# A residual block in fp32 on one core: seven block products for eight in six blocks of the last FFN

## The chip, the core and the metric

The kernel runs on one core of a Trainium2 chip. The time is the device time of one execution in microseconds (us); three executions of the kernel before are given. Engines are named as in the profile: PE (TensorE, matmuls; PEld its weight loads), DVE (VectorE), ACT (ScalarE), POOL (GpSimd) and SP (SyncE, whose queue issues nearly all loads).

## The reference

One layer of a streaming encoder, batch 1, 256 tokens, model width 2048, all in float32. Three sublayers follow one another: an FFN, a mixer (mLSTM heads and RG-LRU channels), and an FFN again. The last is the one that changes:

```python
def _swiglu(u, w13, w2):
    g, v = jnp.split(u @ w13, 2, axis=-1)
    return (jax.nn.silu(g) * v) @ w2
...
mod = (jax.nn.silu(c) @ w_ada[l] + b_ada[l]).reshape(B, N_SUBLAYERS, 3, D_MODEL)
shift, scale, gate = mod[:, :, 0], mod[:, :, 1], mod[:, :, 2]
...
y = _swiglu(modulate(x, 2), ffn2_w13[l], ffn2_w2[l])
x = _layer_norm(ALPHA * x + FFN_WEIGHT * gate[:, 2, None, :] * y, ln_g[l, 2], ln_b[l, 2])
```

`modulate` is a layer norm without gain, times 1 + scale, plus shift. w13 is 2048 x 11264 (5632 columns of g and as many of v), w2 is 5632 x 2048.

## The kernel before

Float32 products are made of three matmuls in a rounded float32 format: each operand is split into a high and a low part, and high x high, high x low and low x high are added in PSUM (`mov_t`, L295). A weight tile is 128 partitions x 2048, 1 MB: 512 rows of K by 512 columns. `load` (L82) has SP fetch it into one of four raw buffers; `split` (L89) has ACT cast it into the high part and DVE subtract that from the raw tile for the low part, in one of three buffer pairs. PE then does 24 matmuls with it: two token halves of 128 (`t`), four K steps of 128, three terms. The activations lie in SBUF as `u2`, transposed and split already (`uh`, `ul`), and are the stationary operand.

The FFN works in blocks of 512 columns of g and the same 512 of v. `rows_block` (L591) does one block: four tiles of K for g, four for v, two PSUM banks each (`fg`, `fv`), then silu(g) x v on ACT and DVE, eight transposes on PE and another split (`gated` L611, `turn` L621) into `hth`, `htl`. Two blocks are a group; there are 11 blocks and six groups, 0 to 5. `g2` (L770) multiplies a group's result with its eight w2 tiles, two for each 512 output columns, and adds the sum into `yacc` in SBUF. In the last FFN the loop at L815 runs `g1(gi)`, the blocks of a group, and then `g2(gi-1)`. The last group but one and the last go through `g2_kept` and `boundary` (L360), which end the kernel.

The vector `mod` comes from 142 further 1 MB tiles, `w_ada`, each a DVE reduction against `scb` (silu(c) on all partitions). `load` calls `tick` (L194), which lets in such an ada tile at a rate per weight tile; for the last FFN this rate is `FFN2_RATE`, and 16 tiles, those of its gate, are left to do there. `gate_rows` (L201) turns the 16 results into a row by a PE transpose, a POOL transfer to DRAM and another back to all partitions, into `gate`. `scale_x` multiplies x by ALPHA on ACT; `residual` (L339) adds gate x yacc to x on DVE.

The order on each engine is set when the program is built, by a scheduler that keeps data dependencies; each engine, and SP's queue, then runs its list strictly in order, and waits where an entry's operand isn't ready.

Of the kernel before, what the change touches and what calls it, by code (L numbers as in the profile page):

```python
# [2 lines left out]

# [13 lines left out]
P = 128  # L17
D = 2048
# [18 lines left out]
RAMP_RATE = (0.75, 0.67, 0.88, 0.6)  # L37
FFN1_RATE = 0.74
MIX_RATE = dict(o=1.2, x=0.8, g=0.4, v=0.4, k=1.25, q=0.5, heads=0.0, out=1.0)
FFN2_RATE = 0.3  # L40

MOD_ACT = (3, 2)

# [8 lines left out]
def block_kernel(ctx: ExitStack, tc: tile.TileContext, a: dict, out: bass.AP):  # L52
# [9 lines left out]
    def slot(name, dtype=F32):  # L62

        return ph.tile([P, SLOT], dtype, tag="slot", bufs=6, name=name)
# [5 lines left out]
    def bank(name):  # L70
        return psp.tile([P, 512], F32, tag="ps", name=name)

    def raw_tile(name):
        return wp.tile([P, 2048], F32, tag="raw", bufs=4, name=name)
# [14 lines left out]
    def split(tile, act, low):  # L89

        raw, name, into = tile
        hi, lo = into() if into else [wp.tile([P, 2048], F32R, tag=w, bufs=3, name=w[0] + name) for w in ("hi", "lo")]
        step = 512 if fine[0] else 2048
        cols = [slice(c, c + step) for c in range(0, 2048, step)]
        for w in cols:
            act.copy(cut(hi, w), like(raw[:, w], hi))  # L96
        for w in cols:
            low.tensor_sub(cut(lo, w), like(raw[:, w], lo), cut(hi, w).bitcast(F32))  # L98
        return hi, lo

    def load_w(src, name, into=None):

        return split(load(src, name, into), nc.scalar, nc.vector)
# [52 lines left out]
            nc.tensor.transpose(ps[:, k * P:(k + 1) * P], col[:, k:k + 1].to_broadcast([P, P]), ident)  # L156


    scb = big.tile([P, D], F32, name="scb")
    sc = cst.tile([P, KT], F32, name="sc")  # L160
    nc.scalar.dma_start(sc, a["c"])
    nc.scalar.activation(sc, sc, AF.Silu)
    for n in range(4):
        ps = bank(f"pc{n}")
        rows_of(ps, sc[:, 4 * n:4 * n + 4])
        nc.scalar.copy(scb[:, n * 512:(n + 1) * 512], ps)
    x = big.tile([P, NT, D], F32, name="x")


    u2 = big.tile([P, KT, 2, S], F32R, name="u2")  # L170
# [2 lines left out]
    badac = cst.tile([P, 3, 3, KT], F32, name="badac")  # L173
    adac = cst.tile([P, 3, 3, KT], F32, name="adac")
    modc = adac[:, :, 0:2, :]
    gate = big.tile([P, D], F32, name="gate")


    todo = list(enumerate(_ada_tiles()))
# [9 lines left out]
    def ada_until(s, j, kt):  # L189

        while any(key == (s, j, kt) for _, key in todo):
            ada_tile()
# [8 lines left out]
    def gate_rows(s, weight):  # L201

        pt = bank(f"adag{s}")
        nc.tensor.transpose(pt[0:KT, 0:P], adac[:, s, 2, :], ident)
        row = sm.tile([KT, P], F32, tag="grow", bufs=1, name=f"grow{s}")
        nc.scalar.mul(row, pt[0:KT, 0:P], weight)
        line = dram.tile([1, D], F32, name=f"line{s}")
        nc.gpsimd.dma_start(line.rearrange("o (k p) -> (o k) p", p=P), row)
        nc.gpsimd.dma_start(gate, line.to_broadcast([P, D]))
# [85 lines left out]
    def mov_t(ps, hl, acth, actl, k0, t, first, last, te=nc.tensor, part=slice(0, 512)):  # L295

        hi, lo = hl
        tk = slice(t * P, (t + 1) * P)
        for j in range(4):
            w = slice(j * 512 + part.start, j * 512 + part.stop)  # L300
            o = like(ps[:, part], hi)
            te.matmul(o, acth[:, k0 + j, tk], cut(hi, w), start=first and j == 0, stop=False)  # L302
            te.matmul(o, acth[:, k0 + j, tk], cut(lo, w), start=False, stop=False)  # L303
            mm = te.matmul(o, actl[:, k0 + j, tk], cut(hi, w), start=False, stop=last and j == 3)  # L304
        return mm
# [3 lines left out]
    def later(tiles, work):  # L309

        pend.append([tiles, work])

    def tile_done(mm):

        for p in pend:
            p[0] -= 1
        while pend and pend[0][0] <= 0:
            with tc.issue_after(mm.ins):
                pend.pop(0)[1]()
# [5 lines left out]
    def mov_w(pss, hl, acth, actl, k0, first, last):  # L325
        for t in range(NT):
            mm = mov_t(pss[t], hl, acth, actl, k0, t, first, last)
        tile_done(mm)
        return mm
# [18 lines left out]
    def scale_x():  # L348
        for t in range(NT):
            A.mul(x[:, t, :], x[:, t, :], ALPHA)  # L350
# [227 lines left out]
        return [sm.tile([P, 5, 6], F32, tag="sts", bufs=2, name=f"sts{s}{t}") for t in range(NT)]  # L578

    def ffn(s, w13, w2, start, following=None):  # L580
        yacc = [slot(f"yacc{t}")[:, 0:D] for t in range(NT)]
        groups = [list(range(g, min(g + GRP, NFF))) for g in range(0, NFF, GRP)]
        hts = {}
# [4 lines left out]
        def new_h(gi):  # L588
            hts[gi] = [slot(f"{w}{gi}", F32R)[:, 0:GRP * S].rearrange("p (a b) -> p a b", a=GRP) for w in ("hth", "htl")]

        def rows_block(b, pg=None, first=None):  # L591

            i = 8 * (b - b0)
            if pg is None:
                pg = [bank(f"fg{s}{b}{t}") for t in range(NT)]
                for k in range(4):
                    mov_w(pg, load_w(w13[i + k], f"fg{s}_{b}{k}"), uh, ul, k * 4, k == 0, k == 3)
            pv = [bank(f"fv{s}{b}{t}") for t in range(NT)]
            for k in range(4):
                if first and k == 0:  # L600
                    tile = first
                else:
                    tile = load(w13[i + 4 + k], f"fv{s}_{b}{k}")
                    with marked():
                        tile = split(tile, nc.scalar, nc.vector)
                mov_w(pv, tile, uh, ul, k * 4, k == 0, k == 3)
            if 4 * b // GRP not in hts:
                new_h(4 * b // GRP)
            gated(b, pg, pv)
# [137 lines left out]
        def g1(gi):  # L747
            grp = groups[gi]
            if start and gi in (2, 3):
                new_h(gi)  # L750
                b = 2 * gi
                later(1, lambda: turn(b, sgs[b]))
                later(3, lambda: turn(b + 1, sgs[b + 1]))
                if gi == 3:
                    later(3, fetch)
                return
            for b in range(grp[0] // 4, grp[-1] // 4 + 1):
                if b or start:
                    rows_block(b)
# [10 lines left out]
        def g2(gi):  # L770
# [3 lines left out]
            for n in range(4):  # L774
# [6 lines left out]
                for t in range(NT):  # L781
                    if gi == 0:
                        evac.append(nc.scalar.copy(yacc[t][:, c], pss[t]))
                    else:
                        nc.vector.tensor_add(yacc[t][:, c], yacc[t][:, c], pss[t])

        ps_last = {}
        behind_t = []

# [15 lines left out]
        if start is not None:  # L805
            ramp(start)
            credit[:] = 0.0, FFN1_RATE
            done = 2
            g2(0)
            flush()  # L810
        else:
            pg, first = nxt.pop()
            credit[:] = -4.0, FFN2_RATE
            rows_block(0, pg, first)
        for gi in range(done, len(groups)):  # L815
            g1(gi)
            if gi == 2 and not start:
                scale_x()
            if gi == len(groups) - 2:
                ada_until(s, 2, KT - 1)  # L820
                gate_rows(s, 0.5)
            if gi == len(groups) - 1:
                g2_kept(gi - 1)
            elif gi:
                g2(gi - 1)
                if gi == len(groups) - 2:
                    for t in range(NT):
                        for n in range(4):
                            residual(s, t, n, yacc[t][:, n * 512:(n + 1) * 512], None)
# [459 lines left out]
```

## Time and profile before

| | |
|---|---|
| median of 3 executions | 1905.65 us (1905.43 to 1908.52) |
| profiled execution | 1905.46 us, its span 1903.7 us |
| busy: PE / PEld / DVE / ACT / POOL | 98% / 81% / 74% / 44% / 2% |
| mean PE clock granted | 0.998 |
| read from HBM, written | 512.36 MB, 2.12 MB |

Busy is the time in which an engine has at least one instruction under way, as a share of the span. PE's matmuls overlap one another, so the sum of their durations is longer than its busy time. In a row of a group of instructions stand the source line, the engine, the operation, what it writes and reads, how often, then its busy time, the mean of one, and the engine's idle time ahead of it with what ended that.

### The profile page before, as it was taken

How to read it: one execution, taken by the hardware profiler on the slowest of the kernel's cores; microseconds unless marked ns; L12 is line 12 of the kernel's file. 1: busy time of each engine (PE TensorE's matmuls, PEld its weight loads, DVE VectorE, ACT ScalarE, POOL GpSimd, SP SyncE). 2: the span in 40 equal slices, each digit the busy share in tenths (PEclk: the TensorE clock that was granted, in tenths of full speed). 3: DMA queues.
4: the chain of work that ended last, by engine and by line, in shares of the span. 5: the costliest groups of instructions: out<-in, count | busy, mean ns of one | idle time of the engine just before them, and what ended most of it. 6: DMA issues, size and time to landing. Idle time of an engine off the chain costs nothing.

```text
span 1903.7 us, 21169 instructions
## 1 busy us (share of the span) xinstructions
PE 1868.8 (98%) x8555; PEld 1540.9 (81%) x8555; DVE 1416.9 (74%) x1358; ACT 845.0 (44%) x792; POOL 43.1 (2%) x64
## 2 busy tenths in 40 slices
PE   6999999999999999999999999999999999999997
PEld 5888888888888888688888786888888888888886
DVE  7899988879877988897998877455655644545657
ACT  5533444443434335657634247434434334343340
POOL 0000000000000000000000120000000000000000
PEclk9999999999999999999999999999999999999999
DMA  9889977888988886696698664566666655555552
GB/s 365 345 331 361 344 291 306 304 352 317 359 344 336 331 338 235 241 347 241 265 360 326 244 268 156 213 224 244 245 260 245 226 196 193 185 197 202 196 218 92
DMA packets 73202, 515.87 MB, mean 271 GB/s; under 512 B 8544, under 2 KB 8720, under 8 KB 11024
## 3 DMA queue, kind: packets, MB, share of 16 engines
q1 hardware_dynamic: 70848, 507.54, 71.1%
q10 hardware_dynamic: 1728, 3.80, 0.6%
q0 software_dynamic: 528, 3.17, 0.4%
q8 instruction: 67, 1.10, 0.2%
q14 instruction: 31, 0.25, 0.0%
HBM read 512.36 MB, written 2.12 MB: 270 GB/s over the span
## 4 chain that ended last, share of the span: by engine, by line
PE 87%; DVE 6%; ACT 2%; DMA 2%; issue 2%; POOL 0%; DVEq 0%; SPq 0%; ACTq 0%
PE py L302 6%; PE py L303 6%; PE py L304 6%; PE fv L302 5%; PE fv L303 5%; PE fv L304 5%; PE fg L302 5%; PE fg L304 5%; PE fg L303 5%; PE rp L690 5%; PE rp L691 4%; PE rp L692 4%; PE pj L291 4%; PE tl L304 3%; PE tl L302 3%; PE tl L303 3%
## 5 line engine op out<-in xcount | busy, mean ns | idle before, releaser
L186 DVE CUSTOM_DVE_ANT_0 ada<-ada,scb,badac 128x2048 f32<-128x2048 f32 x142 | 333.1, 2346 | 22.7 <-DMA ada<-in_w_ada 22.6
L98 DVE TENSOR_TENSOR lw<-rw,hw 128x2048 fp32r<-128x2048 f32 x80 | 183.3, 2291 | 109.5 <-ACT hw L96 109.2
L96 ACT CAST hw<-rw 128x2048 fp32r<-128x2048 f32 x80 | 153.1, 1914 | 238.7 <-PE py L304 128.7
L98 DVE TENSOR_TENSOR lfv<-rfv,hfv 128x2048 fp32r<-128x2048 f32 x55 | 126.0, 2292 | 127.6 <-ACT hfv L96 127.6
L302 PE MATMUL py<-hw,hth 128*128 128x512 f32 x512 | 200.0, 391 | 0.0
L304 PE MATMUL py<-hw,htl 128*128 128x512 f32 x512 | 199.3, 389 | 0.0
L303 PE MATMUL py<-lw,hth 128*128 128x512 f32 x512 | 199.2, 389 | 0.0
L96 ACT CAST hra<-rra 128x2048 fp32r<-128x2048 f32 x63 | 120.6, 1916 | 161.3 <-PE rp L692 112.4
L98 DVE TENSOR_TENSOR lfg<-rfg,hfg 128x2048 fp32r<-128x2048 f32 x52 | 119.1, 2291 | 95.7 <-ACT hfg L96 95.6
L96 ACT CAST hfg<-rfg 128x2048 fp32r<-128x2048 f32 x52 | 99.5, 1914 | 173.7 <-PE fv L304 74.1
L691 PE MATMUL rp<-lra,u 128*128 128x512 f32 x448 | 174.2, 389 | 1.0 <-DVE lra L98 1.0
L96 ACT CAST hfv<-rfv 128x2048 fp32r<-128x2048 f32 x55 | 105.2, 1914 | 156.8 <-PE fg L304 118.0
L692 PE MATMUL rp<-hra,u 128*128 128x512 f32 x448 | 173.6, 389 | 0.0
L690 PE MATMUL rp<-hra,u 128*128 128x512 f32 x448 | 170.8, 392 | 1.7 <-ACT u L259 1.7
L304 PE MATMUL fv<-hfv,u 128*128 128x512 f32 x440 | 171.2, 389 | 0.0
L303 PE MATMUL fv<-lfv,u 128*128 128x512 f32 x440 | 171.2, 389 | 0.0
L302 PE MATMUL fv<-hfv,u 128*128 128x512 f32 x440 | 171.0, 389 | 0.0
L98 DVE TENSOR_TENSOR lra<-rra,hra 128x2048 fp32r<-128x2048 f32 x63 | 144.2, 2289 | 27.5 <-ACT hra L96 27.3
L302 PE MATMUL fg<-hfg,u 128*128 128x512 f32 x416 | 162.3, 390 | 0.0
L304 PE MATMUL fg<-hfg,u 128*128 128x512 f32 x416 | 161.9, 389 | 0.0
L303 PE MATMUL fg<-lfg,u 128*128 128x512 f32 x416 | 161.9, 389 | 0.0
L291 PE MATMUL pj<-u,hs 128*128 128x512 f32 x512 | 123.0, 392 | 0.3 <-ACT hs L96 0.2
(392 smaller groups left out, 3340.9 us busy)
## 6 DMA issues: line engine op xcount, KB each, us to landing
ada<-in_w_ada SPq DMA_DIRECT2D x142, 1024.0 KB, 5.1
rw<-in_w SPq DMA_DIRECT2D x80, 1024.0 KB, 5.0
rra<-in_w_r SPq DMA_DIRECT2D x64, 1024.0 KB, 5.1
rfg<-in_w SPq DMA_DIRECT2D x55, 1024.0 KB, 4.9
rfv<-in_w SPq DMA_DIRECT2D x55, 1024.0 KB, 4.8
rs<-in_w_s SPq DMA_DIRECT2D x32, 1024.0 KB, 7.0
rwo<-in_w_out SPq DMA_DIRECT2D x16, 1024.0 KB, 4.9
rv<-in_w_vo SPq DMA_DIRECT2D x8, 1024.0 KB, 4.8
```

What stands on the lines that cost most here:

```text
L96: act.copy(cut(hi, w), like(raw[:, w], hi))
L98: low.tensor_sub(cut(lo, w), like(raw[:, w], lo), cut(hi, w).bitcast(F32))
L186: vec.tensor_tensor_reduce(raw, raw, scb, 1.0, badac[:, s, j, kt:kt + 1], ALU.mult, ALU.add, adac[:, s, j, kt:kt + 1])
L291: nc.tensor.matmul(ps, hi[:, w], u2[:, k].rearrange("p w b -> p (w b)"), start=k == 0, stop=False)
L302: te.matmul(o, acth[:, k0 + j, tk], cut(hi, w), start=first and j == 0, stop=False)
L303: te.matmul(o, acth[:, k0 + j, tk], cut(lo, w), start=False, stop=False)
L304: mm = te.matmul(o, actl[:, k0 + j, tk], cut(hi, w), start=False, stop=last and j == 3)
L690: nc.tensor.matmul(pss[t], uh[:, k0 + j, tk], hi[:, w], start=a0 and j == j0, stop=False)
L691: nc.tensor.matmul(pss[t], uh[:, k0 + j, tk], lo[:, w], start=False, stop=False)
L692: mm = nc.tensor.matmul(pss[t], ul[:, k0 + j, tk], hi[:, w], start=False, stop=a1 and j == j0 + nj - 1)
```

## The change

In groups 2, 3 and 4 of the last FFN (`MIXED`), so in blocks 4 to 9, `mixed` takes the place of `rows_block`. Of a block's eight w13 tiles four, the first 1024 rows of K for g and v, are multiplied by Strassen's method in Winograd's form. The activations for these rows are a 2 x 2 matrix of parts: two token halves by two K halves of 512. The weights are one as well: two K halves by the columns of g and of v. The eight products of a part with a part (12 matmuls each) become seven, `q1` to `q7`, of which four have sums of activation parts as one operand and four have combined weights. `token_sums` makes the activation sums once, in group 1; they lie in the place of x. The weight combinations are made in each block, in place in the four raw tiles `r`, which `fetch_w` loads one block ahead: `r[0]` into `scb`, `r[1]` into `gate`, the other two into raw buffers. Each operand of a product is split by itself. The other four tiles (`plain`) are done as before. The products' sums go together in SBUF (`wa`, `wb`, `za`, `zb`).

The eight w2 tiles of the group before no longer follow the two blocks; `mixed` takes one at each of four places in each block. Since the sums need x's place, x goes to DRAM behind block 0 and comes back after block 9, and is scaled and given its residual there. Since `scb` and `gate` hold weights, all ada tiles have to be done before group 2 (`FFN2_RATE` 0.58), and the gate row is made after block 9.

```diff
--- before.py
+++ after.py
@@ -37,7 +38,9 @@
-FFN2_RATE = 0.3
+FFN2_RATE = 0.58
+MIXED = (2, 3, 4)
@@ -156,7 +159,7 @@
-    scb = big.tile([P, D], F32, name="scb")
+    scb = big.tile([P, D], F32, tag="scb", name="scb")
@@ -164,7 +167,7 @@
-    x = big.tile([P, NT, D], F32, name="x")
+    x = big.tile([P, NT, D], F32, tag="x", name="x")
@@ -173,7 +176,7 @@
-    gate = big.tile([P, D], F32, name="gate")
+    gate = big.tile([P, D], F32, tag="gate", name="gate")
@@ -578,6 +581,7 @@
     def ffn(s, w13, w2, start, following=None):
+        nonlocal x, gate
         yacc = [slot(f"yacc{t}")[:, 0:D] for t in range(NT)]
         groups = [list(range(g, min(g + GRP, NFF))) for g in range(0, NFF, GRP)]
         hts = {}
@@ -784,6 +788,141 @@
+        def w2_tile(gi, n, k, pss):
+            hth, htl = hts[gi]
+            kg = 2 * gi + k
+            if k == 0:
+                pss[n] = [bank(f"py{gi}_{n}_{t}") for t in range(NT)]
+            mov_w(pss[n], load_w(w2[kg * 4 + n], f"w2{s}_{kg}_{n}"), hth, htl, k * 4, k == 0, k == 1)
+            if k:
+                c = slice(n * 512, (n + 1) * 512)
+                for t in range(NT):
+                    nc.vector.tensor_add(yacc[t][:, c], yacc[t][:, c], pss[n][t])
+        parts = []
+        def token_sums():
+            home = big.tile([P, 2, KT, P], F32R, tag="x", name="sums")
+            ah = raw_tile("usum").rearrange("p (k b) -> p k b", k=8)
+            nc.vector.tensor_add(ah, uh[:, 0:8, :].bitcast(F32), ul[:, 0:8, :].bitcast(F32))
+            a11, a12, a21, a22 = (ah[:, k:k + 4, t * P:(t + 1) * P] for t in range(NT) for k in (0, 4))
+            ss = raw_tile("ssum").rearrange("p (k b) -> p k b", k=KT)
+            s1, s2, s3, s4 = (ss[:, 4 * i:4 * i + 4, :] for i in range(4))
+            nc.vector.tensor_add(s1, a21, a22)
+            nc.vector.tensor_sub(s2, s1, a11)
+            nc.vector.tensor_sub(s3, a11, a21)
+            nc.vector.tensor_sub(s4, a12, s2)
+            sh, sl = home[:, 0], home[:, 1]
+            nc.scalar.copy(sh, ss)
+            nc.vector.tensor_sub(sl, ss, sh.bitcast(F32))
+            parts[:] = sh, sl
+        held = {}
+        def fetch_w(b, j):
+            tag = {0: "scb", 1: "gate"}.get(j)
+            nm = f"b{b}_{j}"
+            t = big.tile([P, 2048], F32, tag=tag, name=nm) if tag else raw_tile(nm)
+            nc.sync.dma_start(t, w13[8 * b + (0, 4, 1, 5)[j]])
+            held[b, j] = t
+        def mixed(b, ws, more):
+            sh, sl = parts
+            r = [held.pop((b, j)) for j in range(4)]
+            def parted(j, nm):
+                return split((r[j], f"{nm}{s}_{b}", None), nc.scalar, nc.vector)
+            def product(ps, hl, acth, actl, k0, t, first, last):
+                tile_done(mov_t(ps, hl, acth, actl, k0, t, first, last))
+            def plain(pss, k, at, first, last):
+                tile_k = load_w(w13[8 * b + at + k], f"f{s}_{b}{at}{k}")
+                for t in range(NT):
+                    mm = mov_t(pss[t], tile_k, uh, ul, 4 * k, t, first[t], last[t])
+                tile_done(mm)
+            def part_bank(nm):
+                return bank(f"{nm}{s}_{b}")
+            def half_tile(tag, nm):
+                return sm.tile([P, 512], F32, tag=tag, bufs=2, name=f"{nm}{s}{b}")
+            sub = nc.vector.tensor_sub
+            add = nc.vector.tensor_add
+            p1 = part_bank("m1")
+            product(p1, parted(0, "q1"), uh, ul, 0, 0, True, True)
+            next(ws)()
+            g = [part_bank("fg0"), part_bank("fg1")]
+            v = [part_bank("fv0"), None]
+            product(g[0], parted(2, "q2"), uh, ul, 4, 0, True, False)
+            plain(g, 2, 0, (False, True), (False, False))
+            product(v[0], parted(3, "q3"), sh, sl, 12, 0, True, False)
+            sub(r[0], r[1], r[0])
+            sub(r[1], r[3], r[1])
+            sub(r[3], r[3], r[0])
+            w0 = half_tile("u", "wa")
+            nc.scalar.copy(w0, p1)
+            next(ws)()
+            p6 = part_bank("m6")
+            product(p6, parted(3, "q6"), sh, sl, 4, 0, True, True)
+            z0 = half_tile("gy", "za")
+            add(z0, w0, p6)
+            plain(g, 3, 0, (False, False), (True, False))
+            sub(r[2], r[2], r[3])
+            if more:
+                fetch_w(b + 1, 3)
+            p7 = part_bank("m7")
+            product(p7, parted(1, "q7"), sh, sl, 8, 0, True, True)
+            z1 = half_tile("gy", "zb")
+            add(z1, z0, p7)
+            next(ws)()
+            if more:
+                fetch_w(b + 1, 1)
+            p5 = part_bank("m5")
+            product(p5, parted(0, "q5"), sh, sl, 0, 0, True, True)
+            add(z0, z0, p5)
+            add(w0, w0, g[0])
+            nc.scalar.activation(w0, w0, AF.Silu)
+            next(ws)()
+            if more:
+                fetch_w(b + 1, 0)
+            product(g[1], parted(2, "q4"), uh, ul, 4, 1, False, True)
+            w1 = half_tile("u", "wb")
+            add(w1, z1, g[1])
+            nc.scalar.activation(w1, w1, AF.Silu)
+            add(z1, z1, p5)
+            v[1] = part_bank("fv1")
+            plain(v, 2, 4, (False, True), (False, False))
+            if more:
+                fetch_w(b + 1, 2)
+            plain(v, 3, 4, (False, False), (True, True))
+            for t, (w, z) in enumerate(((w0, z0), (w1, z1))):
+                add(z, z, v[t])
+                nc.vector.tensor_mul(w, w, z)
+            if 4 * b // GRP not in hts:
+                new_h(4 * b // GRP)
+            later(3, lambda: turn(b, [w0, w1]))
@@ -812,10 +951,31 @@
             pg, first = nxt.pop()
             credit[:] = -4.0, FFN2_RATE
             rows_block(0, pg, first)
+            xd = dram.tile([P, NT * D], F32, name="xd")
+            nc.sync.dma_start(xd, x.rearrange("p t d -> p (t d)"))
         for gi in range(done, len(groups)):
+            if not start and gi in MIXED:
+                pss = {}
+                ws = iter([partial(w2_tile, gi - 1, n, k, pss) for n in range(4) for k in range(2)])
+                if gi == MIXED[0]:
+                    ada_until(s, 2, KT - 1)
+                    for j in (0, 2, 3, 1):
+                        fetch_w(2 * gi, j)
+                for b in (2 * gi, 2 * gi + 1):
+                    mixed(b, ws, b < 2 * MIXED[-1] + 1)
+                if gi == MIXED[-1]:
+                    x = big.tile([P, NT, D], F32, tag="x", name="xb")
+                    gate = big.tile([P, D], F32, tag="gate", name="gateb")
+                    gate_rows(s, 0.5)
+                    nc.sync.dma_start(x.rearrange("p t d -> p (t d)"), xd)
+                    scale_x()
+                    for t in range(NT):
+                        for n in range(4):
+                            residual(s, t, n, yacc[t][:, n * 512:(n + 1) * 512], None)
+                continue
             g1(gi)
-            if gi == 2 and not start:
-                scale_x()
+            if not start and gi == MIXED[0] - 1:
+                token_sums()
             if gi == len(groups) - 2:
                 ada_until(s, 2, KT - 1)
                 gate_rows(s, 0.5)
```

The order on three engines moves as follows; a tile's name ends in the FFN's number 2 and the block (and the K tile), `h` and `l` ahead of it stand for high and low, `r` for raw.

DVE in block 6, first as it was (`lfg` and `lfv` are low parts of w13 tiles, `sg` the gated product, `htl` the low part of its transpose):

```order
L98 TENSOR_TENSOR lfg2_71_10838<-rfg2_71_10835,hfg2_71_10837 128x2048
L617 TENSOR_TENSOR sg260_10797<-sg260_10797,fv260_10673 128x512
L617 TENSOR_TENSOR sg261_10800<-sg261_10800,fv261_10674 128x512
L98 TENSOR_TENSOR lfg2_72_10882<-rfg2_72_10879,hfg2_72_10881 128x2048
L98 TENSOR_TENSOR lfg2_73_10912<-rfg2_73_10909,hfg2_73_10911 128x2048
L98 TENSOR_TENSOR lfv2_70_10944<-rfv2_70_10941,hfv2_70_10943 128x2048
L634 TENSOR_TENSOR htl3_10796<-th60_10865,hth3_10795 128x4x128
L634 TENSOR_TENSOR htl3_10796<-th61_10872,hth3_10795 128x4x128
L98 TENSOR_TENSOR lfv2_71_10974<-rfv2_71_10971,hfv2_71_10973 128x2048
```

and now, from the low part of q2 to that of q6 (`b6_0` to `b6_3` are the four raw tiles `r`):

```order
L101 TENSOR_TENSOR lq22_6_10646<-b6_2_10557,hq22_6_10645 128x2048
L921 TENSOR_TENSOR wa25_10313<-wa25_10313,za25_10364 128x512
L921 TENSOR_TENSOR wb25_10522<-wb25_10522,zb25_10416 128x512
L101 TENSOR_TENSOR lf2_602_10678<-rf2_602_10675,hf2_602_10677 128x2048
L101 TENSOR_TENSOR lq32_6_10706<-b6_3_10397,hq32_6_10705 128x2048
L882 TENSOR_TENSOR b6_3_10397<-b6_3_10397,b6_0_10504 128x2048
L101 TENSOR_TENSOR lw22_5_0_10729<-rw22_5_0_10726,hw22_5_0_10728 128x2048
L638 TENSOR_TENSOR htl2_10181<-th50_10661,hth2_10180 128x4x128
L638 TENSOR_TENSOR htl2_10181<-th51_10668,hth2_10180 128x4x128
L891 TENSOR_TENSOR b6_2_10557<-b6_2_10557,b6_3_10397 128x2048
L101 TENSOR_TENSOR lq62_6_10760<-b6_3_10397,hq62_6_10759 128x2048
```

Between the low parts there now stand subtractions of the same size, and the end of the block before.

ACT around the scaling of x, first as it was, in group 2:

```order
L96 CAST hfv2_52_10203<-rfv2_52_10201 128x2048
L616 ACTIVATE sg251_10267<-fg251_9998 128x512
L121 ACTIVATE x_110<-x_110 128x2048 x2
L96 CAST hfv2_53_10236<-rfv2_53_10234 128x2048
L96 CAST hw22_2_0_10276<-rw22_2_0_10274 128x2048
```

and now, behind block 9:

```order
L99 CAST hfg2_100_12273<-rfg2_100_12271 128x2048
L209 ACTIVATE grow2_12237<-adag2_12235 16x128
L124 ACTIVATE xb_12233<-xb_12233 128x2048 x2
L912 ACTIVATE wb29_12164<-wb29_12164 128x512
L99 CAST hfg2_101_12303<-rfg2_101_12301 128x2048
```

The scaling stands where x has just been sent for, with the casts of block 10 behind it.

SP has two new transfers, here the second with its neighbours (`xd` is the copy in DRAM):

```order
L89 DMA rf2_943_12199<-in_w13_2 128x2048
L89 DMA rfg2_100_12271<-in_w13_2 128x2048
L970 DMA xb_12233<-xd_8657 128x4096
L89 DMA rfg2_101_12301<-in_w13_2 128x2048
L89 DMA rfg2_102_12331<-in_w13_2 128x2048
```

It stands behind the first weight tile of block 10 and ahead of the other seven.

More of the change, by code (lines that the diff above doesn't have):

```diff
@@ L1 @@
 from contextlib import ExitStack, contextmanager
+from functools import partial
 from itertools import chain
```

## The prediction

> **What bounds the kernel now.** I read the page first, for the engine that has no room, then the stretches in which the changed blocks lie, then the start times of single instructions there.
>
> ```profile
> span 1903.7 us, 21169 instructions
> ...
> PE 1868.8 (98%) x8555; PEld 1540.9 (81%) x8555; DVE 1416.9 (74%) x1358; ACT 845.0 (44%) x792; POOL 43.1 (2%) x64
> ...
> PE 87%; DVE 6%; ACT 2%; DMA 2%; issue 2%; POOL 0%; DVEq 0%; SPq 0%; ACTq 0%
> ```
>
> PE is busy for 98% of the span and makes up 87% of the chain of waits. Blocks 4 to 9 of the last FFN and the w2 tiles among them run from about 1384 to 1770 us. The table by stretches of that stage:
>
> ```profile
> core 0: us, PE busy (x) PEld busy (x) DVE busy (x) ACT busy (x) POOL busy (x), PEclk, DMA share, GB/s
> 1380.00:1510.00 130.00, 130.00 (x584) 107.83 (x583) 79.40 (x52) 53.77 (x36) 0.00 (x0) 1.00 0.67 250
> 1510.00:1640.00 130.00, 130.00 (x583) 107.87 (x582) 63.19 (x40) 49.66 (x32) 0.00 (x0) 1.00 0.54 190
> 1640.00:1770.00 130.00, 130.00 (x584) 107.72 (x583) 66.57 (x43) 48.65 (x33) 1.18 (x2) 1.00 0.55 199
> ```
>
> PE is busy in every microsecond of it, at full clock (1.00), with DVE at about half (63 to 79 of 130). So the stage is as long as its row of matmuls, and what a matmul costs is the distance from one start to the next, not its duration. The timeline of PE shows both (start, duration):
>
> ```profile
> 1429.75 0.39 PE L304 MATMUL fg<-hfg,u 128*128 128x512 f32 x1
> 1429.98 0.39 PE L302 MATMUL fg<-hfg,u 128*128 128x512 f32 x1
> ...
> 1431.79 0.39 PE L304 MATMUL fg<-hfg,u 128*128 128x512 f32 x1
> ```
>
> Nine starts in 2.04 us: 0.2267 us each, where the duration column says 0.39, because they overlap. A weight tile feeds 24 matmuls, 5.44 us. The timelines of ACT and DVE, which make the high and low part of each tile, have the same beat:
>
> ```profile
> 1290.34 1.91 ACT L96 CAST hfg<-rfg 128x2048 fp32r<-128x2048 f32 x1 [3.53 <-PE fv L304]
> 1295.78 1.92 ACT L96 CAST hfg<-rfg 128x2048 fp32r<-128x2048 f32 x1 [3.53 <-PE fv L304]
> ...
> 1440.97 2.29 DVE L98 TENSOR_TENSOR lfv<-rfv,hfv 128x2048 fp32r<-128x2048 f32 x1 [3.15 <-ACT hfv L96]
> 1443.18 1.28 DVE L634 TENSOR_TENSOR htl<-th,hth 128x512 fp32r<-128x512 f32 x2
> 1444.38 2.35 DVE L186 CUSTOM_DVE_ANT_0 ada<-ada,scb,badac 128x2048 f32<-128x2048 f32 x1
> ```
>
> The cast begins when PE lets go of one of three buffer pairs, two tiles ahead of need; DVE's 3.15 us of waiting is what 5.44 leaves beside 2.29. It is room, not a loss.
>
> **The change part by part.** *PE.* A block has 8 w13 tiles of 24 matmuls. Half of them, four tiles or 8 block products of 12, become 7 products: 12 matmuls fewer in each of six blocks, 72 in all. 72 x 0.2267 = **16.3 us**. (By the duration column it would be 72 x 0.389 = 28.0 us, which overlap forbids.) Nothing else on PE is added; no idle time in the stage could give more.
>
> [...]
>
> *DVE and ACT, steady blocks.* Four raw tiles were split once each; now seven operands are split (3 casts and 3 low parts more), and four 128x2048 subtractions form the combined weights. Small sums of 128x512 are added. The groups of DVE and ACT in 1380 to 1770 us (count, busy, mean ns, idle before):
>
> ```profile
> L98 DVE TENSOR_TENSOR lfv<-rfv,hfv 128x2048 fp32r<-128x2048 f32 x24 | 55.0, 2293 | 70.5 <-ACT hfv L96 70.5
> ...
> L785 DVE TENSOR_TENSOR yacc<-yacc,py 128x512 f32<-128x512 f32 x21 | 14.4, 684 | 5.5 <-PE py L304 5.5
> ...
> L96 ACT CAST hw<-rw 128x2048 fp32r<-128x2048 f32 x24 | 45.9, 1913 | 84.0 <-PE py L304 52.7 <-PE fv L304 31.3
> ...
> L616 ACT ACTIVATE sg<-fg 128x512 f32<-128x512 f32 x12 | 7.2, 596 | 4.8 <-PE fg L304 4.8
> ```
>
> A 128x2048 subtraction with a plain float result has no row. The nearest are the low part, 2.29, and four pieces of 128x512, 4 x 0.684 = 2.74; I take 2.29, whose size and operands are the same. In the recorded order DVE has between one block's q1 and the next one's 15 low parts and 4 subtractions, 19 x 2.29 = 43.5, and 16 small ones, 16 x 0.684 = 10.9: 54.4 us. PE's share of that block is 7 products of 2.72 and 8 whole tiles of 5.44, 62.6 us, and 0.8 to 0.9 for eight transposes:
>
> ```profile
> 1438.82 1.04 PE L631 MATMUL th<-ident,sg 128*128 128x128 f32 x8
> 1439.61 0.48 PE L302 MATMUL fg<-hfg,u 128*128 128x512 f32 x1
> ```
>
> ACT: 15 casts x 1.91 and 5 small ones x 0.6, 31.7 us. So DVE goes from about half to 86%, ACT to 50%; PE stays the longest.
>
> The mean could hide a tight place, so I take the densest: DVE from behind the low part of a block's last v tile to the low part of q6. There stand 11 large and 8 small operations, 11 x 2.29 + 8 x 0.684 = 30.7 us. PE has over the same places the v tile, q1, a w2 tile, q2, transposes, a g tile, q3 and a w2 tile: 4 x 5.44 + 3 x 2.72 + 0.9 = 30.8 us. That is even. Back to back DVE is a little faster than its durations (1440.97 to 1443.18: 2.21 for a low part, 1444.38 less 1443.18: 0.60 for a small one), which makes it 29.1. The reserve: short and long tiles alternate, so a cast starts 2.72 + 5.44 = 8.16 us ahead of need, less 1.91 and 2.29, which leaves 3.9 us. The other part of the block asks 23.7 of DVE's 32.7 us, so the reserve is refilled in each block. The sums that read PSUM wait for nobody: zb stands behind the low part of q5, done 3.9 us ahead of q5's start, and q5 starts a w2 tile, 5.44, behind the product that zb needs. I take **0** for a steady block, up to 1 us as a bound (DVE 30.7 and a few late semaphores); below 0 is excluded, PE having no idle time to give back.
>
> *The ada tiles move forward.* 16 of them now run with blocks 1 to 3 (rate 0.58 per weight tile, 0.3 before), since their operand's buffer becomes a weight buffer. The stretch with the rate 0.74, in the first FFN, shows what that costs PE:
>
> ```profile
> 430.00:530.00 100.00, 100.00 (x459) 83.15 (x458) 88.27 (x90) 43.44 (x30) 0.00 (x0) 1.00 0.90 344
> ```
>
> PE 100 of 100 us, with DVE at 88% and 344 GB/s. At 0.58 it is 1.58 tiles of 1.05 MB in 5.44 us, 305 GB/s. I take 0. Without that cover each ada tile would cost up to its 2.35 us of DVE.
>
> *The token sums*, once, are 1 large, 4 small, 1 cast and 1 low part, 2 x 2.29 + 4 x 0.684 = 7.3 us on DVE, under block 3's matmuls; but two of the four raw buffers hold them for about three tiles. The landing times (last column):
>
> ```profile
> ada<-in_w_ada SPq DMA_DIRECT2D x142, 1024.0 KB, 5.1
> ...
> rfv<-in_w SPq DMA_DIRECT2D x55, 1024.0 KB, 4.8
> ...
> gate<-line POOLq DMA_DIRECT2D x3, 1024.0 KB, 8.0
> ...
> x<-in_x ACTq DMA_DIRECT2D x2, 1024.0 KB, 9.3
> ```
>
> A buffer turns round in 4.8 + 1.9 + 2.3 = 9.0 us, two give a tile in 4.5; 1.58 are asked for in 5.44, 3.4 us each. Over 16 us that is 3.6 tiles for 4.7 wanted: one late by up to 4.5 us, against a lead of 2 x 5.44 - 4.2 = 6.7. From 0 to 3 us; I take **0.5**, as the lead is the larger.
>
> *x out and back.* The write (2 MB) stands on SP ahead of the last two v tiles of block 0:
>
> ```profile
> 1162.91 11.22 SPq L86 DMA_DIRECT2D rfv<-in_w  x3
> ...
> 1190.42 0.62 PE L302 MATMUL fv<-hfv,u 128*128 128x512 f32 x2
> ```
>
> Those three loads are issued between 1162.9 and 1174.1, and the second is needed a tile after 1190.4, so a transfer of 2 x 9.3 us at the slowest row still fits: 0. The return waits on SP for the last product that reads the sums (q5 of block 9); queued behind it are seven loads of block 10. From q5's end PE has a w2 tile, q4 and two v tiles, 19.0 us, and then the first g tile, loaded ahead of x: 24.5 us until the second. x and that load take 2 x 9.3 + 4.8 = 23.4 at the slowest row, and 6.1 + 4.8 = 10.9 at the 344 GB/s above. But ACT scales x ahead of that tile's cast, and DVE's residual sums wait for the gate rows, which come by two POOL transfers. From 0 to 3 us; I take **0.4**.
>
> *Sum.* The profiled execution took 1905.46 us for a span of 1903.7. 1905.46 - 16.3 + 0.5 + 0.4 = 1890.1, rounded to **1890**. The median of the runs shown, 1905.65, is 0.2 higher, which changes nothing.
>
> **The rivals.** *Small stalls take a part.* The bound of 1 us in each of six blocks and 1 us at either end are 8 us; from a third of that to all of it the time is 1892 to 1897, say 1895. For it speaks the even balance in the densest stretch; against it the 3.9 us of reserve.
>
> *DVE becomes the bound: slower.* In the densest stretch seven low parts stand in a strict row with the subtractions. If cast and low part don't overlap across tiles, each waits 1.91 for its cast: 30.7 + 7 x 1.91 = 44.1, against 30.8 + 3.9; PE loses 9.4 us a block, 56 in all, and the time is 1905.5 - 16.3 + 56 = 1945. It decides from four such waits: 38.3 less 34.7 is 3.6 a block, 22 us, 1911. For it: every low part of before does wait for its cast (70.5 us over 24). Against it: those waits are the 3.15 us that PE's beat leaves over, and ACT is at 50%.
>
> *Nothing gained.* If the ada tiles at 0.58 and the two held raw buffers starve blocks 1 to 3, at 1 us for each of 16 ada tiles, 16 us go and the time is 1906. Against it stands the stretch at 344 GB/s with PE unbroken.
>
> *A matmul is worth less than its beat.* If weight loads and not streams set the pace, at 107.8 us of loads in 130 of the stretch (0.83), a removed matmul is worth 0.188: 13.5 us, 1892. The beat of 0.2267, with weight loads that leave gaps, speaks against it. [...]
>
> **How the numbers follow.** Forecast (stalls under 2 us) 0.63, small stalls 0.21, less per matmul 0.04, nothing gained 0.06, DVE bound 0.06. About 0.2%, 3.8 us, is what a measurement of this kernel can tell from no change. Faster is the sum of the first three, 0.88; same 0.06; slower 0.06. The range: the full 16.3 us, no stall and a run 1 us lower give 1888; the case of small stalls ends at 1897, and 1 us is added for a slower run. Outside are the two rivals without gain and some 0.05 of tails.
>
> **What would show it.** Right: PE 100% in the stretch from 1380 to about 1754, 72 matmuls fewer, the same 0.2267 from start to start, DVE at 85 to 88% there, and the last w2 tiles starting 15 to 16 us sooner. Steps wrong: idle time of PE whose releaser is DVE's low part of q2, q3 or q6 (the dense stretch), a v tile of block 3 (the raw buffers), or the second to fourth g tile of block 10 with ACT waiting for x or DVE for the gate rows. Wrong altogether: DVE busy near 100% in the mixed blocks, or matmul starts further apart while DVE, ACT and DMA all are busier.

## The result and the profile after

The changed kernel takes 1890.51 us (median of four executions, 1889.7 to 1891.85), the kernel before beside it 1906.7 (four executions, 1905.43 to 1908.52): a ratio of 0.9915, 95% interval 0.9898 to 0.9932. The prediction said 1890.

The page of the changed kernel, its span, its busy times and the chain of waits:

```profile
span 1890.1 us, 21168 instructions
...
PE 1852.1 (98%) x8483; PEld 1526.3 (81%) x8483; DVE 1541.1 (82%) x1454; ACT 883.8 (47%) x817; POOL 43.1 (2%) x64
...
PE 86%; DVE 6%; ACT 3%; DMA 3%; issue 2%; POOL 0%; DVEq 0%; SPq 0%; ACTq 0%
```

There are 72 matmuls fewer (8555 to 8483), and PE is still the engine that has no room. The mixed blocks, by stretches:

```profile
core 0: us, PE busy (x) PEld busy (x) DVE busy (x) ACT busy (x) POOL busy (x), PEclk, DMA share, GB/s
1380.00:1510.00 130.00, 130.00 (x580) 107.72 (x579) 103.92 (x66) 64.49 (x41) 0.00 (x0) 1.00 0.53 194
1510.00:1640.00 130.00, 130.00 (x583) 107.83 (x582) 107.33 (x73) 62.47 (x40) 0.00 (x0) 1.00 0.53 194
1640.00:1754.00 114.00, 114.00 (x512) 94.56 (x512) 93.74 (x64) 57.08 (x37) 0.00 (x0) 1.00 0.53 193
```

PE is busy throughout at full clock and keeps its beat: 583 starts in the second stretch, as before. DVE went from 63 to 107 of 130 us there and still holds PE up nowhere. The only wait of PE that is listed from 1180 us to the end (total, times, longest) lies ahead of the mixed blocks:

```profile
PE fg L124 <- ACT u L124: 0.8, 1, 0.8
```

What the last FFN itself gained is read between two fixed points: its first plain product into `fv` and the first matmul on `tl`, behind the mixed blocks. First the kernel before, a row of PE's timeline and one of the view of tile `tl` (durations, then first and last start), then the same of the changed one:

```profile
1184.56 0.79 PE L302 MATMUL fv<-hfg,u 128*128 128x512 f32 x1
...
L302 PE MATMUL tl<-hw,hth x64: 389/389/476, 1825.2 to 1879.8; 128*128 128x512 f32 x64
```

```profile
1186.78 0.79 PE L305 MATMUL fv<-hfg,u 128*128 128x512 f32 x1
...
L305 PE MATMUL tl<-hw,hth x64: 389/389/476, 1811.1 to 1865.7; 128*128 128x512 f32 x64
```

Before it is 1825.2 - 1184.56 = 640.6 us, after 1811.1 - 1186.78 = 624.3. The difference is 16.3 us, 72 x 0.2267. The profiled execution of the changed kernel came 2.2 us later to the first of these points, in code that did not change, so its span is only 13.6 us shorter. Below, "the length of the last FFN" is always this stretch.

### The profile page after: what moved, and what is told of

Read it like the earlier page. It is cut to its first block, busy times and chain, and to the rows that moved or that the text cites. A ratio compares the mean times of both kernels' runs of the same rounds, so it can differ in the third digit from the quotient of the medians.

```text
span 1890.1 us, 21168 instructions
## 1 busy us (share of the span) xinstructions
PE 1852.1 (98%) x8483; PEld 1526.3 (81%) x8483; DVE 1541.1 (82%) x1454; ACT 883.8 (47%) x817; POOL 43.1 (2%) x64
## 4 chain that ended last, share of the span: by engine, by line
PE 86%; DVE 6%; ACT 3%; DMA 3%; issue 2%; POOL 0%; DVEq 0%; SPq 0%; ACTq 0%
PE py L306 6%; PE py L305 6%; PE py L307 6%; PE rp L694 5%; PE rp L695 5%; PE fv L305 5%; PE fv L306 5%; PE rp L696 5%; PE fv L307 5%; PE fg L305 4%; PE fg L306 4%; PE fg L307 4%; PE pj L294 4%; PE tl L305 3%; PE tl L306 3%; PE tl L307 3%
## 5 line engine op out<-in xcount | busy, mean ns | idle before, releaser
L305 PE MATMUL py<-hw,hth 128*128 128x512 f32 x512 | 195.8, 390 | 0.0
L101 DVE TENSOR_TENSOR lq<-b,hq 128x2048 fp32r<-128x2048 f32 x42 | 96.1, 2288 | 55.0 <-ACT hq L99 55.0
L99 ACT CAST hq<-b 128x2048 fp32r<-128x2048 f32 x42 | 80.4, 1913 | 118.3 <-PE py L307 62.7
L307 PEld LDWEIGHTS py<-hw,htl 128*128 128x128 f32 x512 | 96.1, 188 | 20.1
L305 PEld LDWEIGHTS py<-hw,hth 128*128 128x128 f32 x512 | 96.1, 188 | 20.0
L306 PEld LDWEIGHTS py<-lw,hth 128*128 128x128 f32 x512 | 96.1, 188 | 19.6
L294 PEld LDWEIGHTS pj<-u,hs 128*128 128x128 f32 x512 | 94.2, 188 | 19.5 <-ACT hs L99 1.1
L694 PEld LDWEIGHTS rp<-hra,u 128*128 128x128 f32 x448 | 84.0, 188 | 21.1 <-ACT u L262 2.4
L695 PEld LDWEIGHTS rp<-lra,u 128*128 128x128 f32 x448 | 84.1, 188 | 18.5 <-DVE lra L101 1.5
L99 ACT CAST hfv<-rfv 128x2048 fp32r<-128x2048 f32 x31 | 59.3, 1917 | 84.6 <-PE fg L307 63.2
L696 PEld LDWEIGHTS rp<-hra,u 128*128 128x128 f32 x448 | 84.1, 188 | 17.6
```

What stands on the lines that cost most here:

```text
L294: nc.tensor.matmul(ps, hi[:, w], u2[:, k].rearrange("p w b -> p (w b)"), start=k == 0, stop=False)
L694: nc.tensor.matmul(pss[t], uh[:, k0 + j, tk], hi[:, w], start=a0 and j == j0, stop=False)
L695: nc.tensor.matmul(pss[t], uh[:, k0 + j, tk], lo[:, w], start=False, stop=False)
L696: mm = nc.tensor.matmul(pss[t], ul[:, k0 + j, tk], hi[:, w], start=False, stop=a1 and j == j0 + nj - 1)
```

## The experiments

Each starts from the changed kernel and changes one thing in its mixed blocks. The theory: PE's row of matmuls is the whole cost, and DVE has a reserve, by place, beside it. The rivals: the surroundings (x by way of DRAM, the ada tiles, the w2 tiles between) give or take something; only DVE's sum over a block counts; a matmul is worth something other than its beat.

**Eight products in the same surroundings.** In `mixed`:

```diff
-            product(p1, parted(0, "q1"), uh, ul, 0, 0, True, True)
+            whole(g, 0, "q1", 0, True)
...
```

with `whole` splitting a raw tile and multiplying both token halves; the sums `za`, `zb`, `wa` and the four subtractions go, and the places of the next block's loads move with them; all else stays.

> The mixed blocks keep everything of the change (x by way of DRAM, the ada tiles ahead of group 2, the held raw tiles in scb and gate, the token sums, the w2 tiles at four places of each block), but the upper K half is multiplied by the plain eight products instead of seven. My theory, that the whole gain is 72 matmuls at 0.2267 us and all else costs nothing: 16.3 us more than the changed kernel, so the time of the kernel before, within 0.2%. Rival, that alternating with w2 tiles or the earlier ada tiles bring part of the gain: faster than before by some of the 16 us. Rival, that the surroundings cost something which the products pay for: slower than before, by as much as they cost.

Measured 1905.79 us (median of ten) against 1905.66 (13 of the kernel before): ratio 1.0001, 0.9992 to 1.001. The length of the last FFN is 1825.6 - 1185.0 = 640.6 us, that of the kernel before. So everything around the products costs nothing and gives nothing, to within 2 us of time and 0.1 us of this stretch; the gain is the products' alone.

**Two, four and six further large operations of DVE in the densest stretch.** The combined weights are formed several times over (the result is the same):

```diff
             sub(r[0], r[1], r[0])
+            sub(r[0], r[1], r[0])
+            sub(r[0], r[1], r[0])
```

That is the one with two; the one with four does the same for `r[1]`, the one with six has `r[0]` five times and `r[1]` three times in all.

> Each mixed block gets 2 more subtractions of 128x2048 on DVE in the densest stretch (r[0] is replaced by r[1] - r[0] three times, which gives the same value as once). My theory, the stretch with a reserve of 3.9 us: 30.7 + 2 x 2.29 = 35.3 by durations against 30.8 + 3.9 = 34.7, or 29.1 + 2 x 2.21 = 33.5 by start to start: 0 to 0.6 us a block, 0 to 4 us in all over the changed kernel. Rival, no reserve: 4.4 us a block, 27 in all. Rival, only the sum over the block counts: 0.

> 4 more subtractions of 128x2048 in the densest stretch of each mixed block (r[0] and r[1] three times each). Stretch with reserve: 29.1 + 4 x 2.21 = 37.9 or 30.7 + 4 x 2.29 = 39.9 against 34.7: 3.2 to 5.2 us a block, 19 to 31 us over the changed kernel, so slower than the kernel before. Only the sum over the block counts (51.6 + 8.8 = 60.4 or 54.4 + 9.2 = 63.6 of 63.5): 0 to 1 us. No reserve: 7 to 9 us a block, 43 to 55 us.

> 6 more subtractions of 128x2048 in the densest stretch of each mixed block (r[0] five times, r[1] three times). Stretch with reserve: 42.4 or 44.4 against 34.7: 7.7 to 9.7 us a block, 46 to 58 us over the changed kernel. Only the sum over the block counts (64.9 or 68.1 of 63.5): 1.4 to 4.6 us a block, 8 to 28 us. No reserve: 11.6 to 13.6 us a block, 70 to 82 us.

Measured: 1892.01 us with two (ratio 0.9924, 0.9907 to 0.994), 1927.24 with four (1.0115, 1.01 to 1.013), 1956.19 with six (1.0262, 1.0247 to 1.0277): 1.5, 36.7 and 65.7 us over the changed kernel. The 1.5 us alone would not be clear of the spread of these medians; the length of the last FFN, 626.1, 660.6 and 689.7 us against 624.3, gives 1.8, 36.3 and 65.4. With two there is no sign of the 27 us that a stretch without reserve would cost. With four and with six the time is above what my theory said (19 to 31 and 46 to 58 us), and the rows below show why. With two, DVE is at 115.41 of 130 us:

```profile
1510.00:1640.00 130.00, 129.96 (x580) 106.88 (x579) 115.41 (x76) 62.26 (x40) 0.00 (x0) 1.00 0.54 194
```

and the loss is visible almost only in PE's starts: `m<-lq`, the first product with the low part of q6, starts 0.2 to 0.3 us late in each block.

```profile
1538.81 0.61 PE L305 MATMUL fg<-hf,u 128*128 128x512 f32 x2
1539.46 0.50 PE L306 MATMUL m<-lq,sums 128*128 128x512 f32 x1
```

By starts the stretch now asks 29.1 + 2 x 2.21 + 0.60 = 34.1 us (2.21 and 0.60 for a large and a small operation, as in the prediction; the small one is a sum into `yacc`, which the scheduler now puts ahead of q6) against 30.8 + 3.9 = 34.7. So its reserve ends almost exactly at two more operations. The sum over a block is refuted as the rule: with four it is 54.4 + 9.2 = 63.6 us for PE's 63.5, and 6 us a block were lost, not 0.1. PE's waits with four and with six (the row of L124 lies ahead of the mixed blocks):

```profile
PE m L305 <- ACT hq L99: 12.9, 5, 2.7
PE fg L305 <- ACT hf L99: 6.7, 6, 1.3
PE fg L124 <- ACT u L124: 0.8, 1, 0.8
PE m L306 <- DVE lq L101: 0.6, 1, 0.6
```

```profile
PE m L305 <- ACT hq L99: 42.3, 6, 7.9
PE fg L305 <- ACT hf L99: 6.1, 6, 1.0
```

The named releaser is ACT's cast of q6. ACT itself waits for the subtraction that makes q6's operand, in DVE's strict row: with six,

```profile
1562.42 1.90 ACT L99 CAST hq<-b 128x2048 fp32r<-128x2048 f32 x1 [17.01 <-DVE b L888]
```

By starts the stretch asks 29.1 + 6 x 2.21 + 2 x 0.60 = 43.6 us with six (both sums into `yacc` now stand ahead of q6). Against 34.7 that is 8.9 us a block; PE's two waits in a block come to 8.6 to 8.9 us in five blocks and to 4.7 in the first. With four it is 4.4 by the sum, and 3.8 to 4.0 us in five blocks and 0.7 in the first. So the stretch as the prediction drew it, by starts and not by durations, gives PE's waits to within 1 us in every block but the first. But the waits are only 20.2 us of the 36.7 and 48.4 of the 65.7. The rest is a slower PE. The stretch behind one stall, with six, as timeline (some rows left out) and as windows:

```profile
1564.37 0.79 PE L305 MATMUL m<-hq,sums 128*128 128x512 f32 x1 [7.85 <-ACT hq L99]
1566.17 1.22 PE L305 MATMUL fg<-hf,u 128*128 128x512 f32 x2 [1.01 <-ACT hf L99]
...
1568.47 0.63 PE L306 MATMUL m<-lq,sums 128*128 128x512 f32 x1
1568.89 0.63 PE L307 MATMUL m<-hq,sums 128*128 128x512 f32 x1
...
1570.45 0.39 PE L305 MATMUL m<-hq,sums 128*128 128x512 f32 x1
1570.68 0.39 PE L306 MATMUL m<-lq,sums 128*128 128x512 f32 x1
```

```profile
1554.00:1558.00 4.00, 2.52 (x12) 1.74 (x10) 3.87 (x5) 0.00 (x0) 0.00 (x0) 1.00 0.00 0
1558.00:1562.00 4.00, 0.00 (x0) 0.00 (x0) 3.96 (x2) 0.00 (x0) 0.00 (x0) 0.75 0.00 0
1562.00:1564.00 2.00, 0.00 (x0) 0.00 (x0) 1.97 (x2) 1.58 (x1) 0.00 (x0) 0.50 0.00 0
...
1568.00:1570.00 2.00, 2.00 (x6) 1.59 (x5) 2.00 (x2) 0.00 (x0) 0.00 (x0) 0.50 0.69 262
1570.00:1572.00 2.00, 2.00 (x9) 1.61 (x9) 1.89 (x2) 0.25 (x1) 0.00 (x0) 0.93 1.01 422
```

While PE stands here, the granted clock falls from 1.00 to 0.50, and for some 6 us after the stall matmuls start 0.42 us apart instead of 0.227. From 1564.37 to 1570.45 eleven matmuls take 6.08 - 1.01 = 5.07 us where 2.49 would do: 2.6 us more behind this stall. Added up over all of PE's starts in the last FFN, the 65.4 us with six are 48.3 us of waiting, 12.6 us in 59 slow starts like these and 4.4 us in the starts next to the waits. With four the 36.3 us are 20.3, 12.6 (54 starts) and 3.4 us.

**Four further large operations in the loose part of the block**, to see whether the place matters:

```diff
-            if more:
-                fetch_w(b + 1, 1)
             p5 = part_bank("m5")
...
+            for _ in range(4):
+                sub(r[1], r[1], r[2])
             next(ws)()
             if more:
+                fetch_w(b + 1, 1)
                 fetch_w(b + 1, 0)
```

> The changed kernel with four further 128x2048 subtractions a block (they spoil a used-up raw tile, so the output is not the reference's), the same number as in the run with four in the densest stretch, but now between q7 and the block's v tiles. If the tight place is the stretch from behind a block's last v tile to q6, the loose part has 23.7 + 4 x 2.29 = 32.9 us of DVE for 32.7 of PE: between 0 and 3 us over the changed kernel, 1890.5 to 1893.5. If it is the number of large operations a block that costs, wherever they stand, it is 1927 as with the other four.

Measured 1900.3 us (median of nine, 1897.96 to 1904.62; ratio 0.9974, 0.9964 to 0.9984), 9.8 over the changed kernel. In the profiled execution, the slowest of the nine, the last FFN is 14.3 us longer. (`r[1]` is not read again before it is loaded, so nothing of the result hangs on these operations; the expectation is wrong there.) The place matters, 9.8 against 36.7 us, but neither theory's figure came. PE's waits in the profiled execution, and then ACT's:

```profile
PE m L305 <- ACT hq L99: 5.3, 5, 1.1
PE fv L305 <- ACT hf L99: 1.3, 3, 0.9
```

```profile
ACT wb L913 <- DVE wb L912: 35.0, 5, 7.0
...
ACT hf L99 <- DMA rf<-in_w: 9.4, 5, 2.6
```

At the end of each block ACT's Silu of `wb` waits for the last sum of g on DVE, up to 7.0 us (1.1 in the changed kernel). Two casts, which the changed kernel has ahead of the Silu, now stand behind it: that of the last v tile and that of the next block's q1, for which PE waits. The first of them also waits for its load, and my edit had moved a load on SP behind the added operations. (In the changed kernel ACT waits longer for the same load, 22.9 us in five blocks, but there the cast ends about 5 us ahead of the first product with it.) So one more:

**The same four operations on q4's operand**, so that the moved load is back in its place:

```diff
             add(z1, z0, p7)
+            sub(r[2], r[2], r[0])
+            add(r[2], r[2], r[0])
+            sub(r[2], r[2], r[0])
+            add(r[2], r[2], r[0])
             next(ws)()
```

> The changed kernel with four further 128x2048 operations a block in the loose part, as in the run before with four late ones (1900.3), but on the operand of q4 (r[2] less r[0], plus r[0], twice), so that the load of the next block's second raw tile is not held by them on SP; they are spread from behind q6 to q4. If the late loads on SP made the 9.8 us there, this one gives 1890.5 to 1893. If DVE as a strict row is late whatever SP does (the last small sum of g, the Silu on ACT that waits for it, the cast of the last v tile behind that), it stays at 1897 to 1902. If only room over the loose part counts (32.9 us against 32.7), 1890.5 to 1893.5.

Measured 1896.21 us (median of five, 1895.46 to 1899.03; ratio 0.9956, 0.9941 to 0.9971): 5.7 over the changed kernel, between the two expectations. But the added operations read `r[0]` too, so SP's load into its place waits for the fourth of them. SP's waits for an added operation, with four late ones and then here (in the changed kernel no load waits for a subtraction):

```profile
SPq L835 <- DVE b L903: 9.3, 5, 1.9
```

```profile
SPq L835 <- DVE b L901: 12.1, 5, 4.7
```

So this run does not take the loads out of the comparison, and the two theories are not told apart by it. What can be read is which wait ended last. In both kernels DVE comes late to the low part of q4. Its end frees the raw buffer of the block's last v tile, which SP loads from 0.03 us later on; ACT, done with the Silu by then, waits for this load (1.5 to 2.6 us a block with four late operations, 0.7 to 1.8 in four blocks here), and PE waits for the casts behind it. One block of each:

```profile
1573.12 1.91 ACT L99 CAST hf<-rf 128x2048 fp32r<-128x2048 f32 x1 [1.46 <-DMA rf<-in_w]
```

```profile
1632.70 1.91 ACT L99 CAST hf<-rf 128x2048 fp32r<-128x2048 f32 x1 [1.81 <-DMA rf<-in_w]
```

This load takes 6.7 to 7.8 us with four late operations, where SP issues the moved one 2.2 us ahead of it, 4.8 to 6.2 here and 4.8 to 4.9 in the changed kernel. How much of the 4.1 us between the two kernels that makes is open. The 5.7 us that remain (6.6 in the last FFN of the profiled execution) are no single wait: only 1.5 us of PE's waiting are listed in all, and DVE is busy 121.03 of 130 us. Most of them stand in the starts, a few tenths at several places of each block. That stretch of this kernel, and pieces of PE's timeline:

```profile
1510.00:1640.00 130.00, 128.75 (x568) 104.45 (x567) 121.03 (x79) 62.12 (x40) 0.00 (x0) 1.00 0.54 193
```

```profile
1629.10 0.39 PE L307 MATMUL fg<-hq,u 128*128 128x512 f32 x1
1629.50 0.50 PE L306 MATMUL fv<-lf,u 128*128 128x512 f32 x1
...
1636.46 0.50 PE L305 MATMUL m<-hq,u 128*128 128x512 f32 x1 [1.06 <-ACT hq L99]
1636.98 0.50 PE L306 MATMUL fv<-lf,u 128*128 128x512 f32 x1
```

0.40 and 0.52 from start to start instead of 0.23. So the loose part hasn't the 9 us that the sum of durations gave it, and my two parts of a block are too coarse for it: it has a tight place of its own at its end, from the low part of q4 by way of a load to the two casts.

**72 matmuls fewer once more, with DVE and ACT as they are.** Of every second w2 tile's second K part the second token half is left out, once behind p5, once ahead of q6:

```diff
+            short = n in (1, 3)
             for t in range(NT):
+                if not (short and t and k):
                     mm = mov_t(pss[n][t], hl, hth, htl, k * 4, t, k == 0, k == 1 or (short and t == 1))
```

(`n in (0, 2)` for the place ahead of q6.)

> The changed kernel without the second token half of four products of every second w2 tile behind p5 (12 matmuls a block, 72 in all; the output is not the reference's); DVE and ACT do what they did. If PE alone still sets the stage and a matmul is worth its beat, 72 x 0.2267 = 16.3 us go again: 1874.2. If DVE with 54.4 us of 59.9 in the block begins to set it, less goes, 0 to 12 us: 1878 to 1890. [...]

> The same 72 matmuls fewer, but from the w2 tile that stands ahead of q6, in the densest stretch (output not the reference's). PE's 30.8 us there become 28.1, and the lead of q6's cast over its need falls from 3.9 to 2.72 + 2.72 - 4.2 = 1.2 us, so 29.3 stand against 30.7 of DVE by durations (29.1 start to start). If the stretch sets it by durations, 1.4 us a block are lost of the 16.3, 8.4: 1882.6. By start-to-start times nothing is lost: 1874.2, as in the run with the loose place. If only the sum over a block counts, both places give the same time.

Measured 1875.19 us (1873.62 to 1877.58; ratio 0.9841, 0.9825 to 0.9858) and 1872.98 (1872.87 to 1873.57; ratio 0.9828, 0.9814 to 0.9843), the kernel before beside them 1905.51. The length of the last FFN is 608.4 and 608.0 us, 15.9 and 16.3 less than in the changed kernel, so the medians' difference of 2 us lies for the most part in code ahead of it that is the same in both. A matmul is worth its 0.2267 us here too, in the loose place and in the densest. The stretch by durations (8.4 us lost in the second kernel) falls; by start-to-start times (29.1 against 28.1 + 1.2) nothing was to be lost, and nothing was. (A sum into `yacc` stands in that stretch here, which makes it 29.7, so the reserve is some tenths larger than the sum has it.) DVE, busy 111.76 of 130 us in the second kernel, makes no wait of PE.

## Why the prediction was right, point by point

- *72 x 0.2267 = 16.3 us.* Right: 16.3 us in the last FFN, and 15.9 to 16.3 once more for 72 others. The duration column's 28.0 and the 13.5 us of weight loads are refuted by the same number.
- *A plain float 128x2048 subtraction at 2.29 us,* the row I had to borrow. Right. The groups of DVE in the mixed blocks of the changed kernel, where L880 to L891 are the subtractions:

```profile
L101 DVE TENSOR_TENSOR lq<-b,hq 128x2048 fp32r<-128x2048 f32 x42 | 96.1, 2288 | 55.0 <-ACT hq L99 55.0
L101 DVE TENSOR_TENSOR lw<-rw,hw 128x2048 fp32r<-128x2048 f32 x24 | 54.9, 2285 | 2.1 <-ACT hw L99 2.1
...
L882 DVE TENSOR_TENSOR b<-b,b 128x2048 f32<-128x2048 f32 x6 | 13.8, 2292 | 0.2
L880 DVE TENSOR_TENSOR b<-b,b 128x2048 f32<-128x2048 f32 x6 | 13.7, 2285 | 0.0
```

- *Steady blocks 0, DVE at 85 to 88%.* The cost is right: no wait of PE is listed in the mixed blocks. The share is 82% (103.92 + 107.33 + 93.74 of 374 us). I had summed durations; with operations starting 2.21 and 0.60 apart it is 19 x 2.21 + 16 x 0.60 = 51.6 of 63.5 us, 81%.
- *The densest stretch and its 3.9 us.* Right in place and close in size: 29.1 against 34.7 leaves 5.6 us by starts; two more large operations and a small one (5.0) cost 1.5 us in all, four and two small ones stop PE for 3.8 to 4.0 us in all blocks but the first. At two the sum had 0.6 us to spare where q6 was already 0.2 to 0.3 late, so the reserve is about 1 us smaller there than drawn. (8.16 less 1.91 and 2.29 is 3.96 and not 3.9, which changes nothing.) The rival that saw DVE become the bound was wrong on the changed kernel, and its place was right: it comes two to four operations later.
- *The other part of the block, 23.7 of 32.7 us.* Right in that it costs nothing as it is, wrong as a measure of room: 9.2 us more there cost 5.7 to 9.8 us. It counted DVE's time alone and left out that a load and two casts hang on DVE's low part of q4.
- *The ada tiles, x out: 0.* Right; with eight products in the same surroundings the time is that of before. *Token sums 0.5 and x back 0.4:* both 0, since the last FFN is shorter by the full 16.3. For the token sums no wait of PE is listed in block 3, as the lead of 6.7 us had it. On the way back the margin is small. The changed kernel's rows, from the issue of x to the first residual sum:

```profile
1747.67 0.33 SPq L970 DMA_DIRECT2D xb<-xd  x1
...
1757.82 3.70 ACT L124 ACTIVATE xb<-xb 128x2048 f32<-128x2048 f32 x2
...
1764.89 0.56 POOL L212 DMA_DIRECT2D gateb<-line  x1 [6.07 <-DMA line<-grow]
...
1771.08 1.29 DVE L346 TENSOR_TENSOR gy<-yacc,gateb 128x512 f32<-128x512 f32 x2
```

x landed 7.8 us after its issue, 2.3 us ahead of ACT's use of it, where I had taken up to 18.6. The gate row lands 5.0 us after 1764.89, about 1 us ahead of the sum that needs it.

- *The sum, 1890.1, against the profiled 1891.85.* The 0.9 us of stalls did not come; 2.2 us came in the unchanged part ahead of the last FFN and about 0.5 behind it. That the median of 1890.5 lies within half a us of the sum is luck: the stalls that did not come and the other drifts cancel. The last FFN's 16.3 us are no luck. The last w2 tiles started 14.1 us sooner in the profiled execution and not 15 to 16, again by those 2.2 us.

## What to carry to other kernels

Where PE has no idle time, as here, a removed matmul is worth its start-to-start distance (0.2267 us in these kernels), and the engines that pay for it are judged by the densest stretch between two deadlines, by starts and not by durations: here DVE at 82% cost nothing, at 89% about 1.5 us, and twice that extra work 6 to 37 us depending on where it stood. A busy share counts only with the place: look also for a load that waits for a buffer which the second engine frees. Price a stall of PE above its length, since slow matmuls behind it can come on top: here 36.3 us were lost for 20.3 us of waiting. And when PE reads as fully busy, count its starts: 568 instead of 583 in 130 us showed more lost time than the busy column (1.3 us) and the list of waits did.

## What was not expected of the hardware

The stalls of PE cost more than their length: 36.3 us were lost for 20.3 us of waiting with four operations in the densest stretch, 65.4 for 48.3 with six. Behind the stall shown above the granted clock was 0.50, and matmuls started 0.42 to 0.43 us apart. It was not so behind every wait. In the kernel with four late operations PE waited about 1.1 us at the same place in five blocks, with up to 0.9 us just ahead of it. Behind two of these waits, which end at 1510.02 and 1643.28, eight matmuls in a row started 0.42 to 0.43 us apart. Behind the other three, which end at 1444.36, 1576.88 and 1710.39, they started 0.22 to 0.24 us apart from the third on; around the one at 1576.88 the granted clock was 1.00 in every row from 1574 to 1580. One of each kind, from PE's timeline (start, duration):

```profile
1510.02 0.50 PE L305 MATMUL m<-hq,u 128*128 128x512 f32 x1 [1.06 <-ACT hq L99]
...
1511.67 0.63 PE L306 MATMUL fv<-lf,u 128*128 128x512 f32 x1
1512.10 0.63 PE L307 MATMUL fv<-hf,u 128*128 128x512 f32 x1
1512.53 0.63 PE L305 MATMUL fv<-hf,u 128*128 128x512 f32 x1
```

```profile
1710.39 0.50 PE L305 MATMUL m<-hq,u 128*128 128x512 f32 x1 [1.06 <-ACT hq L99]
...
1711.26 0.39 PE L307 MATMUL fv<-hf,u 128*128 128x512 f32 x1
1711.49 0.40 PE L305 MATMUL fv<-hf,u 128*128 128x512 f32 x1
1711.73 0.39 PE L306 MATMUL fv<-lf,u 128*128 128x512 f32 x1
```

Both waits are listed at 1.06 us, and what decides between the two kinds is not shown. The executions of this kernel spread over 6.7 us in nine, those of the changed one over 2.2 in four; only one of the nine was profiled, so where the wider spread comes from is open too.
